# A diffusion backbone on one core: the feed-forward's pool of tiles grows by 384 bytes a partition

## The chip, the cores and the metric

The kernel runs on one core of a Trainium2 chip. The metric is the time of one execution on the device, in microseconds (us); lower is better. TensorE (PE) multiplies, ScalarE (ACT) and VectorE (DVE) do the elementwise work, GpSimd (POOL) a little of it, and SyncE (SP) issues the transfers. A matmul has two instructions: LDWEIGHTS, which loads the 128x128 stationary operand (PEld in the profile), and MATMUL, which streams the moving operand past it (PE in the profile).

## What the reference computes

Two layers on 512 tokens of 1024 channels. Each layer is a mixer and then a SwiGLU feed-forward (FFN); only the FFN matters here:

```
h = h + g1 * mixer(h)                        # layer 0: Fourier + windowed attention, layer 1: pooling
hn = modulate(rms_norm(h), sh2, sc2)
h = h + g2 * ((silu(hn @ w1) * (hn @ w3)) @ w2)     # w1, w3: 1024 x 2816, w2: 2816 x 1024
```

Everything is float32.

## The kernel before

**Three passes.** A product in near-float32 precision is made of three matmuls (`passes`, lines 158 to 161): each operand is split into a high and a low part, and the kernel adds high x high, low weight x high, and high weight x low. Each matmul has a 128x128 stationary weight tile and a moving operand of 512 tokens.

**The feed-forward.** Hidden channels come in 22 tiles, in groups of 8, 8 and 6 (`GROUPS`). For one hidden tile j the kernel takes one unit of `w1` and one of `w3` (each 128x1024) and issues 48 matmuls into `h_ps`: for each of 8 channel tiles three passes with `w1` and three with `w3`. The moving operand is `hnh`/`hnl`, the normalized input. Hidden tile 0 is a special case (`Lead`): its moving operand is `hA`, the scaled input, so that it can begin ahead of the norm's statistics. The activated hidden tiles, split into `ah` and `al`, are then the moving operand of the second product: for each of 8 output tiles one unit of `w2`, with 24 matmuls (18 in the last group) into one accumulator, `w2_ps` in the code and `w_ps` in the profile.

**The weights' stream.** `Stream` hands out weight units in the order of their use: each is loaded into a raw tile, copied by ACT into the high part `w_h`, and DVE subtracts to get the low part `w_l` (line 144). Two units are split ahead. Line 140 chooses where the parts of unit k lie:

```
pool, t = (wp_, "") if alt["pool"] is None or k % 2 == 0 else (alt["pool"], "2")
```

`alt["pool"]` is set to `pf` on line 859, after layer 0's `Lead` has been issued. So units of the mixer, and the four of layer 0's hidden tiles 0 and 1, are all split into the pool `wp_`; from then on even units go to `wp_` and odd ones to `pf` (hidden tile 2 has units 24 and 25, and so on). In the first product that makes `w1` even and `w3` odd; in the second, output tiles take turns, even first.

**Where tiles lie.** A pool lies in one piece in each partition, its tiles one behind the other. `wp_` and then `pb` (with `hnh`, `hnl` and the mixer's `OH`, `OL`) lie ahead of `pf`, and all their tiles are whole multiples of 512 bytes long (2048, 4096 or 8192). The pool `pf` follows; its first two tiles are these (lines 916 and 917), and behind them come `ah`/`al` (and layer 1's `hA`), the odd weight units and the rest:

```
bh = pf.tile([P, 4, 536], F32R, tag="bh", bufs=1, name="bh")
bl = pf.tile([P, 4, 16], F32R, tag="bl", bufs=1, name="bl")
```

`bh` and `bl` are constants of layer 1's pooling mixer: 8576 and 256 bytes a partition, 8832 together, which is 17 times 512 and 128 over. So with addresses counted modulo 512 from the start of `wp_` (the *residue* below), every weight unit in `wp_` and every tile of `pb` has residue 0, and every tile of `pf` behind `bl` has residue 128. The `hA` of layer 0 lies in the mixer's own pool, at residue 448, and the mixer's pools are not touched by the change.

Of the kernel before, what the change touches and what calls it, by code (L numbers as in the profile page):

```python
# [9 lines left out]
F32R = mybir.dt.float32r  # L10
# [6 lines left out]
P = 128  # L17
# [12 lines left out]
def kernel(  # L30
# [33 lines left out]
    def act(out, in_, func=AF.Copy, **kw):  # L64
        return nc.scalar.activation(out=out, in_=in_, func=func, **kw)  # L65
# [3 lines left out]
    def last(engine):  # L69
        return next(q for q in reversed(nc.cur_bb.bb.instructions) if q.engine == engine)  # L70

    def pinned(engine, f, *a):
        """Issues f's work on the engine behind what it has been given so far."""
        with tc.issue_after(last(engine)):
            f(*a)

    def f32(ap):
        return ap.bitcast(F32)
# [4 lines left out]
    def pick(pool, tag):  # L83
        return pb if tag == "tmp" else pool

# [1 line left out]
    cond_sb = cp.tile([P, KT, 2], F32, name="cond_sb")  # L87
    nc.sync.dma_start(out=cond_sb, in_=cond)
    h = cp.tile([P, KT, T], F32, name="h")
# [3 lines left out]
    g_sb = cp.tile([P, 6, KT], F32, name="g_sb")  # L93
    sink_sb = cp.tile([P, 8], F32, name="sink_sb")

# [1 line left out]
    ones = cp.tile([P, P], F32, name="ones")  # L97
    nc.vector.memset(ones, 1.0)
    eps = cp.tile([P, 1], F32, name="eps")
# [14 lines left out]

    condB = cp.tile([P, D], F32, name="condB")

# [1 line left out]
    def raw_tile(n, name):  # L118
        return wp_.tile([P, n], F32, tag="raw", bufs=4, name=name)

    alt = {"pool": None}

    class Stream:
        """Weight tiles in the order of their use: loaded LD tiles and split LS tiles ahead."""

        def __init__(self, units, LD=4, LS=2):
            self.units, self.LD, self.LS, self.raw, self.ready, self.used = units, LD, LS, [], [], 0
# [50 lines left out]
    ada = [cp.tile([P, 48], F32, name=f"ada{l}") for l in range(2)]  # L178

    class AdaCols:  # L180
        """Modulation columns [l][t]: each a product with the broadcast condition, summed along the free axis."""

        def __init__(self, blocks):
            self.tasks = [(l, t) for l, t0 in blocks for t in range(t0, t0 + 8)]
# [19 lines left out]
            self.load(self.done + ahead)  # L204

    class Norm:
        """Statistics of an RMS norm, one 128-channel tile at a time."""

        def __init__(self, pool, n, warm_at=1, sq=("tmp", 8, "tmp", 8), eng=None, direct=1, pool_at=()):
            self.pool_at = pool_at  # L210
# [17 lines left out]
                (self.eng or nc.vector).tensor_tensor(self.parts[0], self.parts[0], s, op=ALU.add)  # L228

        def rstd_cols(self, ps=None):  # L230
            """One column per 128 tokens, which lie on the partitions."""
            if ps is None:
                ps = mm.tile([P, 512], F32, tag="mm", name="nrm_ps")
            nb = self.n // P
            for m, src_ in enumerate(self.parts):
                for b in range(nb):
                    nc.tensor.matmul(ps[:, b:b + 1], src_[:, b * P:(b + 1) * P], ones[:, 0:1],
                                     start=(m == 0 and b == 0), stop=(m == len(self.parts) - 1 and b == nb - 1))
            std = cp.tile([P, nb], F32, tag="stdc", bufs=2, name="std")
            act(std, ps[:, 0:nb], AF.Sqrt, scale=1.0 / D, bias=eps)  # L240
            rs = cp.tile([P, nb], F32, tag="stdc", bufs=2, name="rs")
            nc.vector.reciprocal(out=rs, in_=std)
            return rs
# [22 lines left out]
            return rstd  # L266

    class Lead:
        """First hidden tile of a feed-forward, from h times the scale alone: the reciprocal deviation is applied
        to the product and the shift enters as a column, so that the product needn't wait for the statistics."""  # L270

        def __init__(self, l, A, alloc, wb):
            self.l, self.A, self.alloc, self.hs = l, A, alloc, []
# [81 lines left out]
    ws = Stream([(wf[i], 1024) for i in range(4)] + [wo_unit(dt, half) for half in range(2) for dt in range(KT)]  # L355
                + ffn_units(0) + [(wp[0], 1024), (wp[1], 1024)] + ffn_units(1))

    # =============== layer 0: mixer ===============
    with ExitStack() as es:
        pa = es.enter_context(tc.tile_pool(name="pa", bufs=1))  # L360
        pt = es.enter_context(tc.tile_pool(name="pt", bufs=2))
# [1 line left out]
        def sl(name, n=512, dt=F32, tag="tmp", bufs=8):  # L363
            return pick(pt, tag).tile([P, n], dt, tag=tag, bufs=bufs, name=name)
# [2 lines left out]
        nc.vector.memset(condS, 0.0)  # L367
        act(condS[:, :, 0:2], cond_sb, AF.Silu)

# [1 line left out]
        warm = cp.tile([P, 1], F32, tag="warm", bufs=2, name="warm")  # L371
        act(warm, condS[:, 0, 0:1], AF.Sqrt, scale=0.0)
        nx = Norm(pt, T, warm_at=None, direct=3, pool_at=(1, 4))
# [29 lines left out]
        def mod_rows(kt):  # L403
            ada_rows(adau[kt], misc[:, 0:256], 256)
            rows = sl("rows", n=256)
            act(rows, misc[:, 0:256])
            return rows
# [85 lines left out]
        with tc.issue_after(nx.summed):  # L493
            rows = mod_rows(0)
# [9 lines left out]
        rows = mod_rows(1)  # L504
        for kt in range(KT):
# [7 lines left out]
            if kt + 2 < KT:  # L513
                rows = mod_rows(kt + 2)
# [21 lines left out]
                dft_constants()  # L536
                ws.fill(0)

# [1 line left out]
        KH = [sl(f"KH{i}", n=774, dt=F32R, tag="d3", bufs=8) for i in range(2)]  # L540
        KL = [sl(f"KL{i}", n=774, dt=F32R, tag="d3", bufs=8) for i in range(2)]
        QS = [sl(f"QS{i}", dt=F32R, tag="q", bufs=8) for i in range(8)]
# [67 lines left out]
        SO = [dcon(1, 258 * i, 258) for i in range(2)]  # L610
        RW = dcon(1, 516, 258, rows=2)

# [1 line left out]
        us = []  # L614

        def fourier_in(i):
# [52 lines left out]
            nc.gpsimd.tensor_tensor(YL[:, i, :], y, f32(YH[:, i, :]), op=ALU.subtract)  # L669
            yield  # L670

# [1 line left out]

        def blocks(i):
            return [b for b in (i - 1, i, i + 1) if 0 <= b < 4]
# [26 lines left out]
        def recip(jp, nm, sm):  # L702
            d4 = sl("d4", n=4, tag="d4", bufs=2)
            nc.vector.tensor_tensor(d4.rearrange("p (k j) -> p k j", k=2), nm.rearrange("p (k j) -> p k j", k=2),
                                    sink_sb.rearrange("p (k j) -> p k j", k=2)[:, :, 2 * jp:2 * jp + 2], op=ALU.add)
            e4 = sl("e4", n=4, tag="e4", bufs=2)
            act(e4, d4, AF.Exp)
            s4 = sl("s4", n=4, tag="s4", bufs=2)
            nc.vector.tensor_tensor(s4, sm, e4, op=ALU.add)
            r4 = sl("r4", n=4, tag="r4", bufs=4)  # L710
            nc.vector.reciprocal(out=r4, in_=s4)
            return r4

        def attn_out(i, jp, st):
            """Two heads of either kv group on 128 tokens: probabilities turned and multiplied with the values."""
            kbs = blocks(i) + [4, 5]
            N = len(kbs)
            nm, sm, Ps = st

            def turn(n):  # L720
                tp = mm.tile([P, 512], F32, tag="mm", name="t_ps")
                for c in range(4):
                    nc.tensor.transpose(tp[:, c * P:(c + 1) * P], Ps[c][:, n * P:(n + 1) * P], ident)  # L723
                th = sl("th")
                act(th, tp)
                return th

            ops = mm.tile([P, 512], F32, tag="mm", name="pv_ps")
            th = turn(0)
            r4 = recip(jp, nm, sm)  # L730
            for n in range(N):
                nxt = turn(n + 1) if n + 1 < N else None
                for kv in range(2):
                    nc.tensor.matmul(ops[64 * kv:64 * kv + 64, 0:256], VS[:, kbs[n], kv, :],  # L734
                                     th[:, 256 * kv:256 * kv + 256], start=(n == 0), stop=(n == N - 1),
                                     tile_position=(0, 64 * kv))
                th = nxt
                yield
            rp = ops[:, 256:512]
            for j in range(2):  # L740
                for kv in range(2):
                    c = 2 * kv + j
                    nc.tensor.matmul(rp[64 * kv:64 * kv + 64, j * P:(j + 1) * P],
                                     r4[:, c:c + 1].broadcast_to([P, 64]), ident, start=True, stop=True,
                                     tile_position=(0, 64 * kv))
            rb = sl("rb")[:, 0:256]
            act(rb, rp)
            o = sl("o")[:, 0:256]
            nc.vector.tensor_tensor(o, ops[:, 0:256], rb, op=ALU.mult)
            ov = o.rearrange("p (j t) -> p j t", j=2)  # L750
            oh = OH[:, 2 * jp:2 * jp + 2, i * P:(i + 1) * P]
            act(oh, ov)
            nc.vector.tensor_tensor(OL[:, 2 * jp:2 * jp + 2, i * P:(i + 1) * P], ov, f32(oh), op=ALU.subtract)
            yield
# [85 lines left out]
        run(f_mix, 32)  # L840
        while acol.done < len(acol.tasks):
            acol.step()
# [1 line left out]
        nrm = Norm(pt, T, eng=nc.gpsimd, direct=2)  # L844
        Af = scale_cols(0, 32, 2, "Af0")
        lead = Lead(0, Af, lambda kt, m: sl("hA", n=(512, 640)[m], dt=F32R, tag="qp"[m], bufs=(8, 10)[m])[:, 0:512],
# [6 lines left out]
        rstd = nrm.rstd()  # L853
        lead.product()

    # =============== feed-forward and layer 1 ===============
    pf = ctx.enter_context(tc.tile_pool(name="pf", bufs=2))

    alt["pool"] = pf
# [54 lines left out]

    xs, A1, PX = [], [], []
    bh = pf.tile([P, 4, 536], F32R, tag="bh", bufs=1, name="bh")
    bl = pf.tile([P, 4, 16], F32R, tag="bl", bufs=1, name="bl")

    def pool_band_load(g):
        br = raw_tile(536, "band_r")  # L920
# [5 lines left out]
    pw, shift = [], []  # L926
# [26 lines left out]

    nrm = ffn(0, rstd, Af, lead, pool_in)
    rs_c = nrm.rstd_cols()
# [1 line left out]
    G1 = cp.tile([P, KT], F32, name="G1")  # L957
    nc.vector.tensor_tensor(G1, ada[1][:, 16:24], g_sb[:, 5, :], op=ALU.mult)
    nrm = Norm(pf, T, sq=("sq", 4, "sqa", 1), eng=nc.gpsimd, direct=4)
    # 128 rows of tokens: first and last with the columns up to the middle, inner ones with their 144 columns;  # L960
    # the reciprocal counts are powers of two except at 8 columns on either end, so only those have a low part
    spans = ((0, 0, 256, 0, 0, 0), (3, 256, 512, 136, 504, 8), (1, 120, 264, 392, 0, 0), (2, 248, 392, 392, 0, 0))
    def pool_z(g):
        if g % 2 == 0:
# [54 lines left out]
    lead.product()  # L1019
    rstd = ffn(1, rstd, Af1, lead).rstd()  # L1020

# [1 line left out]
    for kt in range(KT):  # L1023
        o = sf("fo")
        nc.vector.scalar_tensor_tensor(out=o, in0=h[:, kt, :], scalar=g_sb[:, 4, kt:kt + 1], in1=rstd,
# [4 lines left out]
def _host_layout(i):  # L1030
    import numpy as np

    f = np.float32
# [33 lines left out]
    rows = [m[0:512]]  # L1067
# [8 lines left out]
    o["w2a"] = c_(np.stack([np.stack([unit(w2[l][1024 * g:1024 * g + 1024]) for g in range(2)]) for l in range(2)]))  # L1076
    o["w2b"] = c_(np.stack([unit(w2[l][2048:]) for l in range(2)]))

    # constants of the shapes alone
    t = np.arange(T)  # L1080
    inv = (f(10000.0) ** (-np.arange(16, dtype=f) / f(16))).astype(f)
    ang = np.concatenate([(t // 64).astype(f)[:, None] * inv[None], (t % 64).astype(f)[:, None] * inv[None]], axis=1)
# [9 lines left out]
    ce, so = np.cos(2 * np.pi * nk / T) / 256, np.sin(2 * np.pi * nk / T) / 256  # L1092
# [33 lines left out]
```

## Time and profile before

| | |
|---|---|
| time, median of 3 runs | 1022.66 us (1021.63 to 1023.93) |
| span of the profiled execution, first to last instruction | 1020.0 us |
| PE busy | 987.0 us, 97% of the span |
| PEld busy | 783.4 us, 77% |
| DVE / ACT busy | 571.5 us, 56% / 375.3 us, 37% |
| granted TensorE clock, mean | 0.995 of full speed |

The page gives the profiled execution's span and no separate time; the 2.66 us between span and median are taken as what lies around it. Matmuls overlap, so that the busy time of one (some 390 ns) is longer than the step from one to the next (some 230 ns); what a train of matmuls costs is read from the length of a stretch over the number of weight loads in it.

### The profile page before, as it was taken

The page shows a single profiled execution, that of the slowest core. Times are in us where ns is not written, and L with a number is a line of the kernel's source. Part 1 is how long each engine was busy: PE and PEld are TensorE (multiplying, and loading weights), DVE is VectorE, ACT ScalarE, POOL GpSimd, SP SyncE. Part 2 cuts the span into 40 slices and gives each one's busy share as a digit, 9 for nine tenths or more (in the row PEclk, how much of TensorE's full clock was granted, in tenths as well). Part 3 has the DMA queues.
Part 4 walks back from the last instruction along what each step waited for, and adds up shares of the span by engine and source line. Part 5 has one row for each costly group of instructions (what it writes and reads, how often), then busy time and mean ns, then how long its engine had stood idle before and what let it go on. Part 6 is the DMA issues. An engine that isn't in the chain of part 4 may idle for free.

```text
span 1020.0 us, 12270 instructions
## 1 busy us (share of the span) xinstructions
PE 987.0 (97%) x4816; PEld 783.4 (77%) x4816; DVE 571.5 (56%) x903; ACT 375.3 (37%) x595; POOL 26.6 (3%) x27
## 2 busy tenths in 40 slices
PE   5999999999999999999999998999999999999995
PEld 3666777776888888888888888788888888888884
DVE  4678667889866455663554498842332233323234
ACT  4568565455523212322222455532222232213231
POOL 1011001011000000000000001000000000000000
PEclk9999999999999999999999999999999999999998
DMA  9830322653777356673465431133323223322202
GB/s 349 317 103 31 104 63 87 221 168 109 227 245 264 115 176 215 218 235 124 148 214 163 136 104 55 62 92 112 97 92 93 94 83 102 105 83 75 90 1 83
DMA packets 44409, 139.15 MB, mean 136 GB/s; under 512 B 5440, under 2 KB 5568, under 8 KB 44352
## 3 DMA queue, kind: packets, MB, share of 16 engines
q1 hardware_dynamic: 44352, 138.38, 41.5%
q8 instruction: 38, 0.62, 0.3%
q14 instruction: 19, 0.16, 0.0%
HBM read 136.26 MB, written 2.10 MB: 136 GB/s over the span
## 4 chain that ended last, share of the span: by engine, by line
PE 89%; DVE 7%; ACT 2%; issue 1%; DMA 0%; DVEq 0%; SPq 0%; ACTq 0%
PE h_ps L159 16%; PE h_ps L161 16%; PE h_ps L160 16%; PE w_ps L161 8%; PE w_ps L159 8%; PE w_ps L160 8%; PE pv_ps L734 2%; PE t_ps L723 1%; PE mo_ps L159 1%; PE mo_ps L161 1%; PE mo_ps L160 1%; PE s_ps L686 1%; PE s_cx L399 1%; DVE w_l L144 1%; PE s_ps L687 1%
## 5 line engine op out<-in xcount | busy, mean ns | idle before, releaser
L65 ACT ACTIVATE w_h<-w_r 128x1024 fp32r<-128x1024 f32 (+2 forms) x158 | 156.4, 992 | 452.0 <-PE h_ps L161 275.4
L144 DVE TENSOR_TENSOR w_l<-w_r,w_h 128x1024 fp32r<-128x1024 f32 (+2 forms) x158 | 181.1, 1148 | 196.7 <-ACT w_h L65 196.3
L159 PE MATMUL h_ps<-hnh,w_h 128*128 128x512 f32 x672 | 265.5, 395 | 0.0
L161 PE MATMUL h_ps<-hnl,w_h 128*128 128x512 f32 x672 | 264.8, 394 | 0.0
L160 PE MATMUL h_ps<-hnh,w_l 128*128 128x512 f32 x672 | 264.1, 393 | 0.4 <-DVE w_l L144 0.4
L160 PEld LDWEIGHTS h_ps<-hnh,w_l 128*128 128x128 f32 x672 | 126.5, 188 | 30.2 <-DVE w_l L144 0.8
L161 PEld LDWEIGHTS h_ps<-hnl,w_h 128*128 128x128 f32 x672 | 126.2, 188 | 29.9
L159 PEld LDWEIGHTS h_ps<-hnh,w_h 128*128 128x128 f32 x672 | 126.2, 188 | 28.7
L161 PE MATMUL w_ps<-al,w_h 128*128 128x512 f32 x352 | 138.3, 393 | 0.0
L159 PE MATMUL w_ps<-ah,w_h 128*128 128x512 f32 x352 | 138.3, 393 | 0.0
L160 PE MATMUL w_ps<-ah,w_l 128*128 128x512 f32 x352 | 138.2, 393 | 0.0
L198 DVE SCALAR_TENSOR_TENSOR ada_r<-ada_r,condB 128x1024 f32<-128x1024 f32 x80 | 97.6, 1222 | 66.0 <-DMA ada_r<-in_adaR_dram 66.0
L907 DVE SCALAR_TENSOR_TENSOR h<-w_ps,ada,h 128x512 f32<-128x512 f32 x48 | 36.0, 751 | 101.5 <-PE w_ps L161 101.5
L160 PEld LDWEIGHTS w_ps<-ah,w_l 128*128 128x128 f32 x352 | 66.3, 188 | 14.8
L161 PEld LDWEIGHTS w_ps<-al,w_h 128*128 128x128 f32 x352 | 66.2, 188 | 14.8
L159 PEld LDWEIGHTS w_ps<-ah,w_h 128*128 128x128 f32 x352 | 66.2, 188 | 14.7
L65 ACT ACTIVATE ah<-av 128x512 fp32r<-128x512 f32 x44 | 27.8, 632 | 41.5 <-DVE av L893 39.0
L65 ACT ACTIVATE sq<-h 128x512 f32<-128x512 f32 x38 | 23.4, 624 | 30.5 <-DVE h L907 19.8
L896 DVE TENSOR_TENSOR al<-av,ah 128x512 fp32r<-128x512 f32 x44 | 30.2, 686 | 0.7 <-ACT ah L65 0.7
L65 ACT ACTIVATE p<-s_ps,nm 128x512 f32<-128x512 f32 (+1 forms) x32 | 23.6, 737 | 15.2 <-DVE nm L695 15.0
L694 DVE TENSOR_REDUCE mx<-s_ps 128x1 f32<-128x512 f32 (+1 forms) x32 | 24.1, 753 | 8.9 <-PE s_ps L691 8.7
L893 DVE TENSOR_TENSOR av<-si,h_ps 128x512 f32<-128x512 f32 x42 | 28.6, 680 | 0.0
(244 smaller groups left out, 1106.6 us busy)
## 6 DMA issues: line engine op xcount, KB each, us to landing
w_r<-in_w_dram SPq DMA_DIRECT2D x88, 512.0 KB, 3.5
ada_r<-in_adaR_dram SPq DMA_DIRECT2D x80, 512.0 KB, 4.2
w_r<-in_w2a_dram SPq DMA_DIRECT2D x32, 512.0 KB, 4.2
ada_q<-in_adaP_dram SPq DMA_DIRECT2D x32, 256.0 KB, 5.4
w_r<-in_w2b_dram SPq DMA_DIRECT2D x16, 384.0 KB, 3.1
w_r<-in_wo_dram SPq DMA_DIRECT2D x16, 256.0 KB, 2.8
wa_r<-in_wa_dram SPq DMA_DIRECT2D x8, 384.0 KB, 5.7
h<-in_xT_dram SPq DMA_DIRECT2D x4, 512.0 KB, 5.4
```

The source lines that it names most:

```text
L65: return nc.scalar.activation(out=out, in_=in_, func=func, **kw)
L144: nc.vector.tensor_tensor(lo, self.raw[k], f32(hi), op=ALU.subtract)
L159: nc.tensor.matmul(acc, wh, mh, start=start, stop=False)
L160: nc.tensor.matmul(acc, wl, mh, start=False, stop=False)
L161: nc.tensor.matmul(acc, wh, ml, start=False, stop=stop)
L198: nc.vector.scalar_tensor_tensor(out=r, in0=r, scalar=1.0, in1=condB, op0=ALU.mult, op1=ALU.mult, accum_out=ada[l][:, t:t + 1])
L399: nc.tensor.matmul(ps[32 * g:32 * g + 32, :], condS[:, kt, :], r[:, k * n:(k + 1) * n], start=(kt < 4), stop=(kt >= 4), tile_position=(0, ...
L694: nc.vector.tensor_reduce(out=mx, in_=sp[:, lo_:hi_], op=ALU.max, axis=AX.X)
L734: nc.tensor.matmul(ops[64 * kv:64 * kv + 64, 0:256], VS[:, kbs[n], kv, :], th[:, 256 * kv:256 * kv + 256], start=(n == 0), stop=(n == N - ...
L893: nc.vector.tensor_tensor(av, si, hp[:, 512:1024], op=ALU.mult)
L896: nc.vector.tensor_tensor(al, av, f32(ah), op=ALU.subtract)
L907: nc.vector.scalar_tensor_tensor(out=h[:, dt, :], in0=acc, scalar=ada[l][:, 40 + dt:41 + dt], in1=h[:, dt, :], op0=ALU.mult, op1=ALU.add)
```

## The change

`bl` is made 40 columns wide instead of 16; only the first 16 are used as before. It takes 640 bytes a partition instead of 256, and all tiles of `pf` behind it move up by 384 bytes. `bh` and `bl` are now 9216 bytes, 18 times 512: the residue of `ah`, `al`, layer 1's `hA` and the odd weight units goes from 128 to 0. Every engine has the same instructions in the same order with the same waits as before. (The rest of the change is comments that are left out.)

```
-    bl = pf.tile([P, 4, 16], F32R, tag="bl", bufs=1, name="bl")
+    bl = pf.tile([P, 4, 40], F32R, tag="bl", bufs=1, name="bl")
```

Residues of the operands in the feed-forwards, weight / moving:

| matmuls | before | after |
|---|---|---|
| layer 0, hidden tile 0 (`Lead`) | 0 / 448 | 0 / 448 |
| layer 0, hidden tile 1 | 0 / 0 | 0 / 0 |
| all other hidden tiles of layers 0 and 1, `w1`; `w3` | 0 / 0; 128 / 0 | 0 / 0; 0 / 0 |
| layer 1, hidden tile 0 (`Lead`) | 0 and 128 / 128 | 0 / 0 |
| second product, even units (1st, 3rd, ... output tile of a group) | 0 / 128 | 0 / 0 |
| second product, odd units (2nd, 4th, ...) | 128 / 128 | 0 / 0 |

## Rows read from the trace of the kernel before

**Rows 1.** The page: busy us, share, instructions; clock by slice; chain that ended last.

```profile
PE 987.0 (97%) x4816; PEld 783.4 (77%) x4816; DVE 571.5 (56%) x903; ACT 375.3 (37%) x595; POOL 26.6 (3%) x27
...
PEclk9999999999999999999999999999999999999998
...
PE 89%; DVE 7%; ACT 2%; issue 1%; DMA 0%; DVEq 0%; SPq 0%; ACTq 0%
```

**Rows 2.** The page's costliest groups: count, busy us, mean ns of one, idle before.

```profile
L159 PE MATMUL h_ps<-hnh,w_h 128*128 128x512 f32 x672 | 265.5, 395 | 0.0
...
L160 PEld LDWEIGHTS h_ps<-hnh,w_l 128*128 128x128 f32 x672 | 126.5, 188 | 30.2 <-DVE w_l L144 0.8
...
L160 PEld LDWEIGHTS w_ps<-ah,w_l 128*128 128x128 f32 x352 | 66.3, 188 | 14.8
```

**Rows 3.** Waits of PE, 240 to 1020 us: first and last of six.

```profile
PE pl_ps L996 <- ACT zh L65: 1.5, 2, 0.8
...
PE h_ps L160 <- DVE w_l L144: 0.4, 1, 0.4
```

**Rows 4.** Stretches, first product's six long stages: length, PEld busy (loads), clock, DMA.

```profile
263.45:330.21 66.76, 54.13 (x288) 1.00 0.78 255
...
906.61:973.37 66.76, 54.13 (x288) 1.00 0.23 71
sum 445.06, PEld 360.86; mean PEld 60.14
```

**Rows 5.** The same of the second product's six stages.

```profile
330.21:374.45 44.24, 36.13 (x193) 1.00 0.44 137
...
973.37:1006.50 33.13, 26.91 (x143) 1.00 0.00 1
sum 242.90, PEld 198.43; mean PEld 33.07
```

**Rows 6.** Stretches, first four output tiles of layer 0's second product.

```profile
330.21:335.81 5.60, 4.50 (x24) 1.00 0.64 192
335.81:341.30 5.49, 4.50 (x24) 1.00 0.50 172
341.30:346.89 5.59, 4.53 (x24) 1.00 0.29 94
346.89:352.35 5.46, 4.51 (x24) 1.00 0.33 91
```

**Rows 7.** Stretches: layer 0's hidden tiles 0 (part), 1 (part) and 3.

```profile
243.90:250.66 6.76, 5.46 (x30) 1.00 0.69 231
255.07:263.23 8.16, 6.76 (x36) 1.00 0.46 146
...
274.59:285.71 11.12, 9.03 (x48) 1.00 0.90 311
```

**Rows 8.** Stretches of layer 0's output projection (moving `OH`, `OL`, weights in `wp_`).

```profile
226.87:229.19 2.32, 1.88 (x10) 1.00 0.70 217
229.19:234.18 4.99, 4.13 (x22) 1.00 0.64 214
```

**Rows 9.** DVE in order of time, three of its weight splits: start, us.

```profile
257.29 1.22 DVE L144 TENSOR_TENSOR w_l<-w_r,w_h 128x1024 fp32r<-128x1024 f32 x1
...
261.42 1.22 DVE L144 TENSOR_TENSOR w_l<-w_r,w_h 128x1024 fp32r<-128x1024 f32 x1
...
264.07 1.23 DVE L144 TENSOR_TENSOR w_l<-w_r,w_h 128x1024 fp32r<-128x1024 f32 x1 [0.77 <-ACT w_h L65]
```

**Rows 10.** PEld in order of time: first load of hidden tile 3's `w3` low part.

```profile
275.29 0.19 PEld L160 LDWEIGHTS h_ps<-hnh,w_l 128*128 128x128 f32 x1
```

**Rows 11.** Waits of ACT, 655 to 1020 us: us in total, times, longest.

```profile
ACT w_h L65 <- PE h_ps L161: 156.9, 21, 9.4
```

**Rows 12.** Stretch of the pooling mixer, all engines, then clock, DMA.

```profile
622.00:632.00 10.00, 8.25 (x60) 7.61 (x61) 10.00 (x16) 6.41 (x12) 4.00 (x3) 1.00 0.16 52
```

## The prediction

> **What bounds the kernel now.** I read the page first. TensorE is busy for 97% of the span and makes 89% of the chain that ended last [rows 1]; what the change touches, the matmuls of the two feed-forwards, are the costliest groups [rows 2]. Then the waits of PE: from 240 us on there are six entries, the largest 1.5 us in total [rows 3], so PE stands still for nothing there. A feed-forward is one long train of matmuls, and its time is the number of matmuls times the step from one to the next. So the third view is stretches with their weight loads counted. The first product takes 445.06 us for 2 x (288 + 384 + 288) = 1920 matmuls in its six long stages [rows 4], a step of 231.8 ns; the second 242.90 us for 2 x (192 + 192 + 144) = 1056 [rows 5], 230.0 ns. (A row can count one load more or less than the program has, at its border.) The clock is at its upper level, 2.4 GHz, in each of these rows, so 512 columns of moving operand would take 512 / 2.4 = 213 ns. The step is longer, though nothing waits for another engine. A weight load takes 188 ns in either product [rows 2], and the rest of the step is what a change of addresses could reach.
>
> **Does the step depend on the residues?** The kernel before holds the comparison already. In the second product output tiles take turns: same matmuls, same accumulators, and only the weights' residue changes. Residue 0 against a moving 128: 5.60 and 5.59 us for 24 loads, 233 ns. Residue 128 against 128: 5.49 and 5.46 us, 228 ns [rows 6]. Unequal residues cost 5 to 6 ns a matmul. The pool is not the cause: hidden tile 1 of layer 0 has its weights in the other pool, at 0 against 0, and its undisturbed part takes 8.16 us for 36 loads, 226.7 ns. Hidden tile 3, with `w3` at 128 and moving 0, takes 11.12 us for 48, 231.7 ns [rows 7], although only half of its matmuls have unequal residues; in turns of three passes the equal ones don't get the short step either. A third distance, `hA` at 448 against 0, gives 6.76 us for the 29 steps between its 30 loads, 233 ns [rows 7]. The output projection, 0 against 0 throughout, shows why short trains hide this: ten loads after a stop take 2.32 us, 232 ns each, and the next 22 take 4.99 us, 226.8 ns [rows 8]. With equal residues a train settles on 226.7 ns after some ten matmuls and stays there; any other pair keeps it at 231 to 233.
>
> **What the change does, part by part.**
>
> *First product.* All of it gets 0 / 0, as hidden tile 1 has now, and that row holds the same pattern of two weight units in turns, two accumulators in turns, and three passes. At 226.7 ns the 1920 matmuls take 435.3 us instead of 445.06: 9.8 us less. Hidden tile 1 of layer 1 lies outside those stages: 48 x 5.0 ns = 0.2 us. Hidden tile 1 of layer 0 is unchanged.
>
> *Second product.* 1056 x 226.7 ns = 239.4 us instead of 242.90: 3.5 us, most of it from the even output tiles, a little from the odd ones, which now begin each tile unsettled.
>
> *`Lead` of layer 1.* 48 matmuls from 128 to 0; at the price of other unequal pairs about 40 of them, those not held by a wait, gain 5 ns: 0.2 us.
>
> *Pooling mixer.* Some of its matmuls (96 into `z_ps`, 80 into `pl_ps`, of 256 columns and fewer) change residues. In its widest part DVE is busy for 10.00 of 10 us and PE for 8.25 [rows 12], so I put this at nothing, with DVE's work as the cover; without that cover, 5 ns on each is 0.9 us either way.
>
> *ACT and DVE.* Their tiles in `pf` move too. The parts of odd units are written at another residue, one ACT and one DVE instruction a unit. These finish far ahead: in layer 0 the nearest case after hidden tile 2 is the low part of tile 3's `w3` (unit 27, the last of these three splits), written by 264.07 + 1.23 = 265.30 us [rows 9] and loaded at 275.29 [rows 10], 10 us of margin; in layer 1 ACT waits 156.9 us for PE to give weight tiles back [rows 11], so it is PE that sets the pace. A hidden tile takes 0.24 us less after the change, 20 of them in layer 0 under 5 us, which these margins hold. Price: nothing.
>
> *Sum.* 9.8 + 0.2 + 3.5 + 0.2 = 13.7 us. The profiled span of 1020.0 becomes 1006.3, and the median, 2.66 above it, 1009.0. The other bound takes the step from the odd output tiles as they are, with their settling: 5.46 / 24 = 227.5 ns. Then the first product gains 1920 x 4.3 = 8.3, the second 242.90 - 240.2 = 2.7, and with the 0.4 of the small terms it is 11.4 us, 1011.3. I take the settled step, since nothing in the feed-forwards stops PE [rows 3], and the change of unit and accumulator every 12 matmuls in [rows 8] did not unsettle the train.
>
> A rule of the Trainium skill speaks against any of this. "TensorE: Matmul & The Clock Gate", Part 2, says at the step on LDWEIGHTS that TensorE has two independent read ports, and that loading the next weights takes no bandwidth from the running matmul. By that rule the residues could not matter and the time would stay at 1022.7; the alternating rows of the second product disagree with it by 5 to 6 ns a matmul.
>
> **The rivals.**
>
> *Settled only in part.* A train may come unsettled at each accumulator's start when 41 hidden tiles and 48 output tiles follow each other with other work around. Ten matmuls at 232 instead of 226.7 ns are 0.05 us, times 89 starts 4.7 us; the gain shrinks to 9.0 and the time is 1013.7. For it: each odd output tile now begins slower, which makes its 227.5. Against it: those tiles come behind one with unequal residues, and afterwards none does.
>
> *No change.* What differs between output tiles could be what else runs beside them, since ACT and DVE work in a rhythm of two units, or the ports of that rule are independent after all: 1022.7. Against it: the rows at 226.7 are from two other places, with other neighbours [rows 7, 8].
>
> *Slower.* The raw tiles, the high and the low parts, `ah` and `al` and all that PE reads would stand at one residue, where now half of what ACT and DVE write lies at another. If their accesses held up PE's, each train would stay unsettled at the worst step seen, 233 ns: (1920 + 48) x 1.3 = 2.6 us on the first product, 1056 x 3.0 = 3.2 us on the second, 1028.5. It decides as soon as the mean step of the 2976 matmuls passes today's (445.06 + 242.90) / 2976 = 231.2 ns. Against it: while hidden tile 1 ran at 226.7 ns, DVE was splitting units 24 and 26 from raw tiles into `wp_`, all at residue 0, from 257.29 and 261.42 us on [rows 9].
>
> **How the numbers follow.** The settled case has 0.83, the partly settled 0.10, no change 0.04, slower 0.03. The forecast is 1009.0. Its own bounds are 1009.0 and 1011.3; the pooling mixer's 0.9 us either way and the three runs of before, which lie 1.0 below and 1.3 above their median, make that 1007.3 to 1013.3. Toward the partly settled case I take it up to 1013.7, and leave the other two outside. A measurement of this kernel can tell some 0.2% (2 us) from no change; the first two cases lie beyond that, so faster has 0.93, same 0.04, slower 0.03.
>
> **What the profile after would show.** If the steps are right: each stage of 288 loads of the first product at about 65.3 us instead of 66.76, of 384 at 87.1; output tiles of the second product no longer in turns, all 24 loads in 5.44 us; `w_h` still waiting for PE; PE's waits as short as now; layer 0's `Lead` still at 233 ns. The prediction is wrong if hidden tiles stay at 11.1 us with equal residues, if the short step shows only in the second product, or if PE begins to wait for `w_l`.

## The result, and the profile after

The time went from 1022.14 us (median of 4 runs beside those of the changed kernel) to 1007.65 us (1007.3 to 1008.66, 4 runs): a ratio of 0.9861, 95% interval 0.9847 to 0.9875. That is 14.5 us where 13.7 were forecast, and inside the range of 1007.3 to 1013.7. The span of the profiled execution is 1005.2 us.

The page of the changed kernel, the lines that answer to [rows 1, 2]:

```profile
PE 971.7 (97%) x4816; PEld 781.0 (78%) x4816; DVE 571.7 (57%) x903; ACT 375.7 (37%) x595; POOL 26.6 (3%) x27
...
PEclk9999999999999999999999999999999999999998
...
L159 PE MATMUL h_ps<-hnh,w_h 128*128 128x512 f32 x672 | 261.6, 389 | 0.0
...
L160 PEld LDWEIGHTS w_ps<-ah,w_l 128*128 128x128 f32 x352 | 66.1, 188 | 13.7
```

PE is still busy for 97%, the weight load still takes 188 ns, DVE and ACT have the same work. Only the matmul became shorter, 389 instead of 395 ns, and that is the modelled duration, not the step. The step is read from the stretches, as before the change: length, busy time of the weight loads and their count, clock, DMA share, GB/s. First product, six long stages, against [rows 4]:

```profile
262.58:327.86 65.28, 54.05 (x288) 1.00 0.74 250
371.38:458.42 87.04, 72.07 (x384) 1.00 0.67 225
...
893.84:959.12 65.28, 54.07 (x288) 1.00 0.23 73
sum 435.20, PEld 360.42; mean PEld 60.07
```

Second product, against [rows 5], and its first four output tiles, against [rows 6]:

```profile
327.86:371.38 43.52, 36.04 (x192) 1.00 0.46 155
...
959.12:991.77 32.65, 26.85 (x143) 1.00 0.00 1
sum 239.37, PEld 198.04; mean PEld 33.01
```

```profile
327.86:333.30 5.44, 4.50 (x24) 1.00 0.88 298
333.30:338.74 5.44, 4.50 (x24) 1.00 0.53 184
338.74:344.18 5.44, 4.50 (x24) 1.00 0.27 96
344.18:349.62 5.44, 4.50 (x24) 1.00 0.29 96
```

The alternation of 5.60 and 5.46 us is gone: 65.28 / 288 = 87.04 / 384 = 5.44 / 24 = 226.7 ns a matmul in every stage and every tile.

Feeding is no tighter. PE's waits from 237 us on are six entries as before (the first, here 2.9 us, was 2.8 over the same stretch before), and ACT still waits for PE to give weight tiles back ([rows 3, 11]):

```profile
PE nrm_ps L251 <- ACT sq L65: 2.9, 2, 1.7
...
PE h_ps L160 <- DVE w_l L144: 0.4, 1, 0.4
```

```profile
ACT w_h L65 <- PE h_ps L161: 151.8, 21, 9.1
```

**What is not the change's.** Layer 0's `Lead`, whose residues are as they were, took 14.6 us from its first matmul to the next tile's before and 13.2 after. The clock explains it. In the profiled execution of before, a stretch there ran in part at the lower of the two clock levels, 1.2 GHz, with a mean of 0.73 of full speed, the first row; the same place in the changed kernel, the second, has none:

```profile
237.20:243.60 6.40, 4.57 (x31) 0.73 0.01 3
```

```profile
237.60:243.40 5.80, 4.35 (x35) 1.00 0.02 6
```

Such a stretch comes and goes with the execution: the kernel with the raw tiles moved, below, has the changed kernel's residues in all that PE reads and shows it at this place (0.74 from 236.5 to 243.0 us), with a `Lead` of 14.6 us, and the one with the mixer moved shows one at 620 to 630 us instead (0.83). The first long stage begins 0.87 us earlier (262.58 against 263.45) although nothing ahead of it was changed. So some 0.9 us of the 14.8 between the two spans is chance of these two executions.

### The profile page after: what moved, and what is told of

The parts are those of the page before. It is cut to its first block, busy times and chain, and to the rows that moved or that the text cites. A ratio compares the mean times of both kernels' runs of the same rounds, so it can differ in the third digit from the quotient of the medians.

```text
span 1005.2 us, 12270 instructions
## 1 busy us (share of the span) xinstructions
PE 971.7 (97%) x4816; PEld 781.0 (78%) x4816; DVE 571.7 (57%) x903; ACT 375.7 (37%) x595; POOL 26.6 (3%) x27
## 4 chain that ended last, share of the span: by engine, by line
PE 86%; DVE 7%; ACT 2%; DMA 2%; issue 1%; DVEq 0%; SPq 0%; ACTq 0%
PE h_ps L160 16%; PE h_ps L161 16%; PE h_ps L159 16%; PE w_ps L159 8%; PE w_ps L161 8%; PE w_ps L160 8%; DMA ada_r<-in_adaR_dram 2%; PE pv_ps L734 2%; PE t_ps L723 1%; DVE w_l L144 1%; PE s_cx L399 1%; PE s_ps L686 1%; PE q_ps L159 1%; DVE nrm_u L326 1%; PE mo_ps L159 1%
## 5 line engine op out<-in xcount | busy, mean ns | idle before, releaser
L159 PE MATMUL h_ps<-hnh,w_h 128*128 128x512 f32 x672 | 261.6, 389 | 0.0
L161 PE MATMUL h_ps<-hnl,w_h 128*128 128x512 f32 x672 | 261.4, 389 | 0.0
L160 PEld LDWEIGHTS w_ps<-ah,w_l 128*128 128x128 f32 x352 | 66.1, 188 | 13.7
L159 PEld LDWEIGHTS w_ps<-ah,w_h 128*128 128x128 f32 x352 | 66.1, 188 | 13.7
```

The lines of the kernel that those rows point to most:

```text
L159: nc.tensor.matmul(acc, wh, mh, start=start, stop=False)
L160: nc.tensor.matmul(acc, wl, mh, start=False, stop=False)
L161: nc.tensor.matmul(acc, wh, ml, start=False, stop=stop)
```

## The experiments

Each is a short edit of the changed kernel; residues are addresses modulo 512 counted from the weights' pool, as in the part before the prediction. Each ratio is taken to runs of the kernel before on the same chip.

**1. Another distance: 256.** `bl` 24 columns wide puts the pool's tiles at residue 256.

```
-    bl = pf.tile([P, 4, 40], F32R, tag="bl", bufs=1, name="bl")
+    bl = pf.tile([P, 4, 24], F32R, tag="bl", bufs=1, name="bl")
```

> The tiles of the pool pf behind bl stand at residue 256 instead of 0 (before: 128). Theory (a train settles at 226.7 ns a matmul only where weight and moving operand share their address modulo 512): as before the change, hidden tiles 11.12 us, even output tiles of the second product 5.59 us, odd ones 5.46 us, time 1022 us. Rival (the period is 256 or shorter): hidden tiles 10.88 us, all output tiles 5.44 us, time 1008 us.

Measured: 1008.29 us, ratio 0.9871 (0.9843 to 0.9900). A hidden tile, then an even and an odd output tile:

```profile
272.98:283.86 10.88, 9.01 (x48) 1.00 0.90 298
327.38:332.82 5.44, 4.50 (x24) 1.00 0.72 218
332.82:338.26 5.44, 4.50 (x24) 1.00 0.52 181
```

The theory as written falls, and the rival holds: a distance of 256 bytes between weight and moving operand is as good as none, in either product. What counts is the distance modulo 256. The change's 384 bytes bring the operands to one address modulo 512, but that is more than is needed.

**2. Distance 64.** The same edit with 44 columns: the pool's tiles at 64.

> The tiles of pf behind bl at residue 64. Theory (equal modulo 512): as before the change, hidden tiles 11.12 us, even output tiles 5.59, odd 5.46, time 1022 us. Rival (a period of 64, or closeness counts: the nearer the addresses, the smaller the loss): hidden tiles between 10.88 and 11.0 us, even output tiles below 5.52, time 1008 to 1015 us.

Measured: 1022.01 us, ratio 1.0002 (0.9991 to 1.0013): no change of the time, as the theory said. The rows (a hidden tile, an even output tile, an odd one) hold one thing that it did not say:

```profile
286.30:297.44 11.14, 9.01 (x48) 1.00 0.71 239
463.82:469.33 5.51, 4.51 (x24) 1.00 0.38 105
469.33:474.79 5.46, 4.51 (x24) 1.00 0.53 185
```

The even tile, weights at 0 and moving at 64, takes 5.51 us, 229.6 ns a matmul, less than at 128 (5.59); that is below the 5.52 which the rival set for it. Hidden tiles, in turns of 0 / 0 and 64 / 0, take 232.1 ns, and there the rival fails. So the sign of the distance matters; the sweep below goes on from here.

**3 and 4. One side at a time.** A pad, requested behind the activations' first tile, parts them from the odd weight units. In the first kernel the activations go to 0 and odd units stay at 128 (pad of 32 columns); in the second the activations stay at 128 (`bl` of 16 columns) and odd units go to 0 (pad of 96).

```
                 a.append((ah, al))
+                if l == 0 and j == 0:
+                    pf.tile([P, 32], F32, tag="pad", bufs=1, name="pad")
```

> A pad of 128 bytes between the activations and the odd weight units in pf: ah, al and layer 1's hA at residue 0, odd units at 128. Theory (the pair of operands counts): hidden tiles stay at 11.12 us (weights 0 and 128 in turns against moving 0); in the second product the roles change, the even output tiles, now 0 / 0, take 5.46 us or less, the odd ones, 128 / 0, 5.59; time 1022 us. Rival (odd units are the faster ones by their pool or by the work beside them): odd 5.46, even 5.59 as before.

> A pad of 384 bytes between the activations (which stay at 128, bl as before) and the odd weight units, which go to 0. Theory: every hidden tile is 0 / 0 and takes 10.88 us, 9.9 us less in all; every output tile is 0 / 128 and takes 5.59 us (4.19 in the last groups), 1056 x 232.9 ns = 245.9 us instead of 242.9, 3.0 more; time 1022.4 - 6.9 = 1015.5 us. Rival (what counts is that all that ACT and DVE write stands at one residue): no hidden tile below 11.1, time 1022 us.

Measured: 1021.45 us, ratio 1.0000 (0.9988 to 1.0011), and 1015.35 us, ratio 0.9946 (0.9924 to 0.9969). With the activations moved, a hidden tile, then four output tiles, even first:

```profile
273.53:284.65 11.12, 9.02 (x48) 1.00 0.87 286
329.16:334.64 5.48, 4.50 (x24) 1.00 0.58 188
334.64:340.23 5.59, 4.52 (x24) 1.00 0.46 177
340.23:345.69 5.46, 4.50 (x24) 1.00 0.30 96
345.69:351.28 5.59, 4.53 (x24) 1.00 0.30 91
```

With the odd units moved, a hidden tile and two output tiles:

```profile
274.36:285.24 10.88, 9.01 (x48) 1.00 0.82 293
328.76:334.35 5.59, 4.50 (x24) 1.00 0.71 218
334.35:339.95 5.60, 4.50 (x24) 1.00 0.46 168
```

The roles of even and odd tiles change when the moving operand alone moves: the pool of a weight, or the work beside it, is not what makes it fast. And the two products come apart: with the odd units alone moved, the first product has all of its gain, while in the second the odd tiles rise from 5.46 to 5.60 us and the even ones stay. The rival of the second kernel falls too: its activations, which ACT and DVE write, stand at 128, and its hidden tiles still take 10.88 us. The pair of PE's own operands decides, and the times are those forecast within 0.6 us.

**5. The other engines' operand.** The raw tiles, which ACT and DVE read, get lengths that put their four buffers at four residues.

```
-        return wp_.tile([P, n], F32, tag="raw", bufs=4, name=name)
+        return wp_.tile([P, 1056], F32, tag="raw", bufs=4, name=name)[:, 0:n]
```

> The changed kernel, with the raw tiles (which ACT and DVE read to split) 128 bytes longer, so that their four buffers stand at residues 0, 128, 256 and 384; all that PE reads stays at 0. Theory (only PE's own two operands count): hidden tiles 10.88 us, output tiles 5.44, time 1008 us, as the changed kernel. Rival (the other engines' reads belong to it, and a common residue keeps them out of PE's way): steps back above 228 ns, hidden tiles over 10.94 us, time 1012 us or more.

Measured: 1009.16 us, ratio 0.9873 (0.9855 to 0.9892). A hidden tile from 273.95 to 284.83 us takes 10.88, an output tile from 328.35 to 333.79 us 5.44, to the hundredth as in the changed kernel. Where ACT and DVE read their raw tiles plays no part.

**6 and 7. The other distances.** The odd units' buffers get a length of 4128 bytes, so that three of them stand 32 bytes apart in residue, and a pad that lets the low parts stand as the high ones do; `bl` of 42 and 46 columns sets the activations at 32 and 96. (In the second kernel the first pad is 48 columns instead of 8.)

```
...
+                m = 1032 if t else n
+                if t and not pads:
+                    pads.append(pool.tile([P, 8], F32, tag="pad0", bufs=1, name="pad"))
-                hi = pool.tile([P, n], F32R, tag="whi" + t, bufs=3, name="w_h")
+                hi = pool.tile([P, m], F32R, tag="whi" + t, bufs=3, name="w_h")[:, 0:n]
...
+                if len(pads) == 1:
+                    pads.append(pool.tile([P, 104], F32, tag="pad1", bufs=1, name="pad"))
...
```

> Distances swept in one kernel: the activations stand at 32, so that even output tiles have weight minus moving address 224 modulo 256; the three buffers of odd units stand at 64, 96 and 128, so that odd output tiles have 32, 64 and 96 in turns. Theory (after the run at 256: equal modulo 256 settles at 226.7 ns; every other distance costs 2.5 to 6.5 ns more): output tiles of 24 loads at 5.50 to 5.60 us for each of the four distances, none at 5.44 or below. Rival (a train's step is set by how far apart the two streams are, and some distance is shorter still, towards 512 / 2.4 = 213 ns): at least one distance below 5.44 us.

> The rest of the distances: the activations stand at 96, even output tiles at distance 160; odd output tiles at 192, 224 and 0 in turns. Theory: the tiles at 0 take 5.44 to 5.47 us (after an unequal neighbour), those at 192 about 5.49 as with the pool at 64, the others 5.50 to 5.60. Rival (some distance is shorter still): one of them below 5.44 us.

Measured: 1024.85 and 1023.81 us, one run each. Output tiles of the first kernel, at distances (weight minus moving, modulo 256) of 224, 32, 96 and 64:

```profile
462.36:467.96 5.60, 4.50 (x24) 1.00 0.42 107
467.96:473.56 5.60, 4.51 (x24) 1.00 0.52 177
479.15:484.77 5.62, 4.52 (x24) 1.00 0.30 93
490.36:495.96 5.60, 4.51 (x24) 1.00 0.27 94
```

Of the second, at 160, 192, 0 and 224:

```profile
462.29:467.89 5.60, 4.51 (x24) 1.00 0.42 118
467.89:473.40 5.51, 4.51 (x24) 1.00 0.47 169
479.00:484.47 5.47, 4.51 (x24) 1.00 0.30 96
490.06:495.66 5.60, 4.50 (x24) 1.00 0.26 94
```

Of the eight distances at steps of 32 bytes only two stand out: 0 without a loss, and 192 with about 40% of it. (The tile at 64 in the second experiment had its weight 64 bytes below the moving operand, which is 192.) The others, 128 among them by the kernel before, all lie at 5.59 to 5.62. None is shorter than equal residues: the rival falls, and with it the hope of a better distance at these steps.

**8. The mixer too.** 64 bytes of pad ahead of the mixer's tiles bring layer 0's `hA` and others from 448 to 0.

```
-        perm_sb = pa.tile([P, P], F32, name="perm_sb")
+        perm_sb = pa.tile([P, P + 16], F32, name="perm_sb")[:, 0:P]
```

> The changed kernel, with 64 bytes of pad ahead of the mixer's tiles, so that layer 0's hA, the key and value weights and the attention's queries go from residue 448 to 0 as well. Theory: layer 0's Lead goes from 233 to 227 ns a matmul where nothing holds it (some 40 x 6.5 ns = 0.26 us), the 48 key and value matmuls of the input projection gain up to 5 ns each (0.24 us), the trains beside them settle a little oftener: 0.3 to 1.0 us less than the changed kernel, 1007.2 us, which the clock of runs can hardly tell; the Lead's stretch in the profile can. Rival (in the mixer the steps are short trains between waits, and nothing settles): no difference at all, Lead included.

Measured: 1009.47 us (1006.95 to 1012.55, 5 runs), ratio 0.9881 (0.9864 to 0.9898); the span of the profiled execution is 1004.9 us, 0.3 less than the changed kernel's. In an undisturbed part of the `Lead`, the changed kernel and this one:

```profile
246.90:250.35 3.45, 2.77 (x16) 1.00 0.48 170
```

```profile
245.80:249.20 3.40, 2.82 (x16) 1.00 0.54 165
```

A border of a row can cut a load in two, so the step is read from the matmuls' starts in the trace: they go in steps of 231 and 236 ns in the first and of 225 to 228 in the second, once it has settled after some ten. The whole `Lead` takes 13.2 and 13.0 us. So the mechanism holds there as well, but the time of runs doesn't show it: the median is 1009.47 us where 1007.2 were expected and the changed kernel has 1007.65.

**9. One load in three.** Pads of 128 bytes before and 384 behind the low parts, in either pool, set `w_l` alone at 128.

```
...
+                pad(pool, 32, "pad1" + t)
                 lo = pool.tile([P, n], F32R, tag="wlo" + t, bufs=3, name="w_l")
+                pad(pool, 96, "pad2" + t)
...
```

> The changed kernel with pads of 128 and 384 bytes around the low parts of the weights in both pools, so that w_l alone stands at residue 128: one load in three is unequal. Theory (an unequal operand unsettles the train around it, as w3 alone did in the kernel before, where half of the loads unequal kept all steps at 231.8 of 233 ns): mean step 230 to 232 ns, hidden tiles 11.04 to 11.13 us, output tiles 5.52 to 5.57, time 1017 to 1022 us. Rival (each load pays for itself): 226.7 + 6 / 3 = 228.7 ns, hidden tiles 10.98 us, output tiles 5.49, time 1013.7 us.

Measured: 1021.25 us, ratio 0.9998 (0.9984 to 1.0011). A hidden tile and an output tile:

```profile
272.74:283.84 11.10, 9.08 (x48) 1.00 0.86 282
328.21:333.76 5.55, 4.54 (x24) 1.00 0.70 204
```

231.2 ns a matmul, as the theory had it: one unequal load in three costs 4.5 of the 6 ns on the average of all three. Two thirds of right addresses bring almost nothing.

**10 and 11. Fewer columns.** The kernel before, with the second product on fewer tokens: on 256, then on six other counts, one for each group. The sums of the other tokens are left out, so that only the steps are compared and not the times (909.63 and 974.55 us, one run each).

```
+            nt = ((448, 384, 320), (480, 416, 288))[l][gi]
...
-                passes(acc, (wh[:, s_], wl[:, s_]), a[j], j == 0, j == nj - 1)
+                passes(acc[:, 0:nt], (wh[:, s_], wl[:, s_]), [q[:, 0:nt] for q in a[j]], j == 0, j == nj - 1)
...
```

> The kernel before (pool as it was, residues 0 and 128), with the second product of either feed-forward on 256 of the 512 tokens; the other half of its sums is left out. Even output tiles are 0 / 128, odd ones 128 / 128, 24 matmuls of 256 columns each. Theory (a fixed cost per matmul, 13.3 ns over the columns' time and some 6 more where the residues differ): odd tiles 24 x 120.0 = 2.88 us when settled, even ones 24 x 126 = 3.02 us. Rival (the cost of unequal residues goes with the columns streamed): odd 2.88, even 24 x 123 = 2.95 us. Second rival (the weight load, 188 ns, bounds it): both at 4.5 us.

> The kernel before, with the second product on fewer tokens, another number in each group: 448, 384 and 320 columns in layer 0, 480, 416 and 288 in layer 1; the sums of the other tokens are left out. Even output tiles are 0 / 128, odd ones 128 / 128. The run at 256 columns showed 120.0 ns at equal residues and 118.3 at unequal ones, so the cost at 512 (6 ns) is neither fixed per matmul nor in proportion to the columns. Theory (the cost is paid where the moving operand's stream sets the step: columns / 2.4 GHz + 13.3 ns when settled, which is 213.3, 200.0, 186.7, 173.3, 146.7 and 133.3 ns for 480 to 288 columns; unequal residues add to it, the more the longer the stream): equal tiles on that line, unequal ones 3 to 7 ns above it down to 384 columns and near it at 288. Rival (only the full 512 columns, a whole accumulator, pay): unequal tiles on the line at every count.

Measured at 256 columns: output tiles with unequal, equal and again unequal residues (each is 24 matmuls; the count of loads takes in the neighbours'):

```profile
339.75:342.59 2.84, 2.84 (x26) 1.00 0.62 189
342.59:345.47 2.88, 2.88 (x26) 1.00 0.59 186
345.47:348.31 2.84, 2.84 (x26) 1.00 0.54 185
```

At equal residues 120.0 ns, as forecast; at unequal ones 118.3, *less*. None of the three expectations holds for the unequal ones. At other counts, an unequal tile and an equal one each of 448, 384 and 480 columns:

```profile
330.50:335.38 4.88, 4.51 (x24) 1.00 0.57 196
335.38:340.25 4.87, 4.51 (x24) 1.00 0.64 183
467.06:471.28 4.22, 4.22 (x25) 1.00 0.41 147
471.28:475.44 4.16, 4.16 (x25) 1.00 0.37 121
706.11:711.33 5.22, 4.50 (x24) 1.00 0.41 111
711.33:716.53 5.20, 4.50 (x24) 1.00 0.56 188
```

With 384 columns equal residues give 4.16 / 24 = 173.3 ns, exactly columns / 2.4 GHz + 13.3, and unequal ones 2.5 ns more. With 448 and 480 the unequal tile costs about 1 ns more, but the equal one itself is some 3 ns above that line. With 320 either takes 2.64 us for 18 matmuls, 146.7 ns, on the line; with 288 the unequal ones are on it (2.40 us for 18, 133.3 ns) and the equal ones below (2.37 us, 131.7). Neither the theory nor its rival is right: the loss does not simply grow with the stream, and it is not there for 512 columns alone.

## Why the prediction was right

**The step per matmul: right to the hundredth of a microsecond.** The forecast took 226.7 ns from 36 matmuls of hidden tile 1 [rows 7] and from the settled part of the output projection [rows 8]. The first product was to take 435.3 us and took 435.20; the second 239.4 and took 239.37. Experiments 1, 3 and 4 show that it is the pair of addresses that does it.

**The sum.** First product 445.06 - 435.20 = 9.9 us (forecast 9.8); second 242.90 - 239.37 = 3.5 (3.5). Layer 1's hidden tile 1 went from 11.23 to 11.02 us, 0.2 (0.2). Its `Lead`, from the first matmul behind the mixer's last (at 638.80 us before, 631.15 after) to the next tile's (651.26, 643.46), went from 12.46 to 12.31, 0.15 (0.2). Together 13.75 against 13.7. The second product's sum in [rows 5] is 0.15 us short: its third stage ends at 607.55 us, where the next matmul starts, and was read to 607.40. So its gain is rather 3.7 and the total 13.9, which with the 0.87 us ahead of the first long stage makes the 14.8 of the spans. The 0.8 us by which the medians differ more than forecast lies inside their interval (12.8 to 15.6 us).

**The choice of the settled step over 227.5 ns: right.** No output tile begins unsettled any more; the partly settled case, 1013.7, did not come about.

**What was put at nothing.** The margins of ACT and DVE held: PE waits 0.4 us for a low part, as before. Where the other engines read has no part in it (experiment 5), which takes the ground from the rival on the slower side. The pooling mixer, from the last output tile's end to layer 1's `Lead`, gained nothing that could be seen: the two executions are 7.68 us apart at its beginning (607.55 and 599.87) and 7.65 at its end (638.80 and 631.15).

**What was not right.** The modulus of the residues: 512 is not the period, 256 is (experiment 1). The forecast did not depend on it. "Any other pair keeps it at 231 to 233" was too strong: a weight 64 bytes below the moving operand gives 229.6 ns in the second product (experiments 2 and 7), and one 96 above it 234 (experiment 6).

**What lies around the span.** The 2.66 us that the forecast adds to the span were a median and a span of different executions. Wherever the time and the span of one execution are both known, they are 2.0 to 2.2 us apart (1007.3 and 1005.2 for the changed kernel); the same sum with 2.1 gives 1008.4. The median of the kernel before was 1022.66 us then and 1022.14 beside the changed kernel, which is the same half microsecond. So the gain was forecast well, but the time is 1.35 us below the forecast and only 0.35 above the range's lower bound, and that it stayed inside is in part luck. The prediction's terms for its bounds also add up to 1007.1 and 1013.5, not to 1007.3 and 1013.3; the measured time lies inside either.

**The weight load.** The Trainium skill, "TensorE: Matmul & The Clock Gate", Part 2, step on LDWEIGHTS, has it that loading the next weights takes no SBUF read bandwidth from the running matmul. At equal addresses modulo 256 nothing in this case speaks against it: the load's 188 ns lie within a step of 226.7. At other addresses the case disagrees: 512 columns take 2.9 to 7.5 ns a matmul more (experiments 6 and 7), so the two reads are not independent.

**Open.** How the two reads meet was not seen, only that their distance modulo 256 decides at 512 columns. Why counts of 288, 416, 448 and 480 columns are off the line even at equal residues, and why 256 columns run faster at unequal ones, stays open. Steps finer than 32 bytes were not run.

## What to carry to other kernels

Where a trace shows one long train of matmuls with nothing waiting, read the step from stretches with their loads counted, tile by tile: tiles of the same shape that differ by 2% in turns point to where their operands lie. For 512 columns of float32r, let every weight tile and every moving tile stand at one address modulo 256; pads of a few hundred bytes do it, and one operand of three left out spoils most of the gain. A comparison that the kernel already contains, here one tile and a short train, can price a change closely (13.7 us forecast, 14.5 measured); the same rule at another count of columns has to be measured anew.

## What the runs showed of the hardware that was not expected

- Period of 256 bytes: a distance of 256 in half of a hidden tile's matmuls gives 10.88 us a tile, 0 gives the same, 128 in half of them gives 11.12.
- Of the eight distances at steps of 32 bytes only 0 (226.7 ns settled) and 192 (229.6 ns) are below 232 ns in output tiles.
- At equal addresses a train needs about ten matmuls after a stop to settle (232 ns each [rows 8]), and then goes on without a change: all 24-load tiles of the second product take 5.44 us.
- Settled steps are columns / 2.4 GHz + 13.3 ns at 512, 384, 320 and 256 columns (226.7, 173.3, 146.7, 120.0); at 448 and 480 equal residues give 202.9 and 216.7 instead of 200.0 and 213.3, at 288 they give 131.7 instead of 133.3.
- At 256 columns the weight load's own 189 ns do not bound the step of 120: loads overlap each other.
